# A two-layer encoder on one core: layer norms centred early on a partial mean, and two more tiles begun on the first half of the tokens

## The chip, the cores and the metric

The kernel runs on one core of one Trainium2 chip. A core has a matrix engine (PE, which multiplies a stationary 128x128 block with up to 512 moving columns and adds up in PSUM), three engines for elementwise work (VectorE or DVE, ScalarE or ACT, GpSimd or POOL) and SyncE (SP), which here issues the transfers. The metric is the device time of one execution in microseconds (us), the median of several runs.

## The reference

The input is 512 tokens of 1024 features in fp32; sixteen meta tokens go ahead of them, so 528 tokens run through two layers. Cut to what matters here:

```
h = layer_norm(concat(meta, x))
for l in range(2):
    cq, ckv, kr, lru_g, lru_x, g_mla, g_lru = split(h @ w_in[l])
    y_mla = attention(rms(cq), rms(ckv), rope(kr)) @ w_o_mla[l]
    y_lru = (gelu(lru_g) * rg_lru(dwconv(lru_x))) @ w_o_lru[l]
    z = sigmoid(g_mla) * y_mla + sigmoid(g_lru) * y_lru
    h = layer_norm(ALPHA * h + z @ w_out[l])
    gate, val = split(dwconv3(h @ w_up[l]))
    h = layer_norm(ALPHA * h + (gelu(gate) * val) @ w_down[l])
return h[16:]
```

`layer_norm` takes mean and variance over the 1024 features of a token, variance as the mean of the squared centred values. The hidden width of the second half is 2 x 2816; ALPHA is the constant weight of the residual.

## The kernel before

Features lie on the partitions: an activation is eight tiles x0 to x7 of 128 features by 528 tokens. Precision is kept by splitting every operand into a high part and a low rest (`split`: a cast, then a subtraction), so one block of weights times one tile is three matmuls, high x high, low x high and high x low (`unit`). A tile of 128 output features takes 8 blocks, for the two halves of the tokens (256 and 272, later 270 and 258 columns, as one PSUM bank holds 512) 48 matmuls. Weights come by DMA as `raw` in lots of 1024 columns, and are split on the chip into `whi` (ACT or DVE) and `wlo` (DVE or POOL); `Weights.take` does that.

All instructions are collected first and then put in order by a list planner (`Core.order`), which keeps PE's order as written, places the others by guessed costs and by times by which PE needs them, and picks the engine where an operation allows two ("VG": DVE or POOL). PSUM is a pool `d` of three double banks (`banks`, `pair`) and a pool `s` of two single banks (`bank`). In gaps that it expects, it places dummy matmuls (L361, `warm`).

A layer norm works across partitions: PE multiplies a tile with a matrix of ones, so that every partition gets the sum over all features. Three layer norms stand between two stages of matmuls; at these places the kernel works by halves of the tokens. `last_tiles` runs the last matrix ahead of the norm (w_out or w_down): tiles 0 to 3 over all tokens, then tiles 4 to 7 (`plt1`) for the first half, then for the second. `post` adds a finished tile to x, `add` adds x up in `lnsum`. After each half `ln_chunk` makes the norm: PE sums lnsum (bank `lnm`), eight centrings x - mean on DVE, eight squares on ACT, four additions, PE sums the squares (`lnv`), then eps, reciprocal and square root (`lnrs`), then per tile a scaling on DVE (g times lnrs), a cast to the high part (`h1h`; after w_down `h2h`) and the low part (`h1l`, `h2l`). Behind the norm `mtiles_by_chunk` begins the next stage with three tiles, first half of the tokens first: after w_out `pfg`, `pfv`, `pfg` (w_up), after w_down and at the start `pckv`, `pcq0`, `pcq1` (w_in). At the start the tokens' own norm (`ln0`) and its transposes (`ln0p`, from the input tiles `xin`) come in two halves too, the second popped from `later` after the first tile.

After pckv, pcq0 and pcq1 comes the tile `pkr` (the shared rotary key), times the tables cos and sin in `kra`, `krb`; then `rms` normalizes ckv and cq (`rrs`), and `rpa` is the first matmul tile on normalized queries. The tiles `pg` of the gates g_lru stand there as cover, others follow in the recurrent stage, whose order LRU_PLAN writes out ("L3" is g_lru's fourth tile). `conv3` and `ffn_post` make the hidden features f from a pair of tiles of w_up.

Of the kernel before, what the change touches and what calls it, by code (L numbers as in the profile page):

```python
# [43 lines left out]
            "L3 x6 O7 t2 x7 g4 y4 g5 y5 g6 g7 t3 y6 y7 l4 l5 l6 l7").split()  # L44
# [482 lines left out]
def trunk_kernel(ctx: ExitStack, tc: tile.TileContext, x, meta, wblk, vecs, rope, ident_in, lnf, out):  # L527
# [123 lines left out]
    for l in range(DEPTH):  # L651
# [45 lines left out]
        def ln_chunk(xs, s, c, g, b, hn):  # L697
            a, e = c
            n = e - a
            pm = bank("lnm")[:, :n]  # L700
            K.mm([(pm, ones, s[:, a:e], True, True)])
            K.act(small("dummy"), ones[:, 0:1], AF.Sqrt)
            qs = []
            for m in range(KD):
                xm = xs[m][:, a:e]
                K.stt(xm, pm, -1.0 / D, xm, ALU.mult, ALU.add)
                q = U("lnsq", F32, (128, n))
                K.act(q, xm, AF.Square)
# [4 lines left out]
            pv = bank("lnv")[:, :n]
            for m, q in enumerate(qs):
                K.mm([(pv, ones, q, m == 0, m == len(qs) - 1)])
            rs = U("lnrs", F32, (128, n))
            K.ts(rs, pv, 1.0 / D, LN_EPS, ALU.mult, ALU.add)
            K.recip(rs, rs)
            K.act(rs, rs, AF.Sqrt)
            for m in range(KD):  # L720
                xm = xs[m][:, a:e]
                hi, lo = hn[m][0][:, a:e], hn[m][1][:, a:e]
                K.stt(xm, xm, vec((g, l), m), rs, ALU.mult, ALU.mult)
                K.affine(hi, xm, 1.0, vec((b, l), m))
                K.stt(lo, xm, vec((b, l), m), hi.bitcast(F32), ALU.add, ALU.subtract)
            if g == "ln1_g":
                for m in range(KD):
                    K.affine(xs[m][:, a:e], xs[m][:, a:e], 1.0, vec((b, l), m))

        def last_tiles(name, xs, n_full, ks, kin, post, g, b, hn, cs):  # L730
# [51 lines left out]

        pss = [banks("pckv"), banks("pcq0"), banks("pcq1")]
        mtiles_by_chunk(pss, [kd("ckv", 0), kd("cq", 0), kd("cq", 1)], h, CF)
# [11 lines left out]
        pk = pair("pkr")  # L796
        mtile(pk, kd("kr", 0), h, CF)
        ta, tb = U("kra"), U("krb")
        K.tt(ta[0:64], pk[0:64], cos4[0:64], ALU.mult)
        K.tt(tb[0:64], pk[64:128], sin4[64:128], ALU.mult)  # L800
# [8 lines left out]
        sg, sg2, z1 = {}, {}, {}  # L809
# [174 lines left out]
        pre = chain([gate("g_lru", m, sg2) for m in range(3)])  # L984
# [124 lines left out]
        for m in range(KD):  # L1109
# [13 lines left out]
                   lambda m, ps, sl: residual(x1[m], ps, sl), "ln1_g", "ln1_b", hn, CQ)  # L1123
# [15 lines left out]
        def ffn_post(j, pg, pl):  # L1139
            sl = slice(FA, T)  # L1140
            tg = conv3(pg, j, "fg")
            K.act(tg[:, sl], tg[:, sl], AF.Gelu_apprx_tanh)
            tv = conv3(pl, NJ + j, "fv")
            K.tt(tg[:, sl], tg[:, sl], tv[:, sl], ALU.mult)
            f[j] = split_new(tg, "f", sl)

        def ffn_up(j):
# [8 lines left out]
        ffn_post(0, pg, pl)
        pl1 = pair("pfv")
        mtile(pl1, kd("w_up", NJ + 1), h, CQ)
        ffn_post(1, pg1, pl1)

        if not last:
# [9 lines left out]
            for j in range(2, PARTS[0].stop):  # L1171
                ffn_up(j)
            for p in range(1, 4):
# [7 lines left out]
                for j in PARTS[p - 1]:  # L1181
# [4 lines left out]
                       lambda m, ps, sl: K.tt(x1[m][:, sl], x1[m][:, sl], ps, ALU.add), "ln2_g", "ln2_b", hn, ((0, MIDS[1]), (MIDS[1], T)))  # L1186
# [64 lines left out]
        for j in range(2, NJ, 2):  # L1251
            ffn_up(j)
# [118 lines left out]
```

## Time and profile before

| | |
|---|---|
| median of 3 runs | 1839.12 us (1837.47 to 1840.18) |
| the profiled execution, its own time | 1835.23 us |
| its span, first to last instruction | 1833.5 us |
| PE busy | 97% of the span |
| DVE, ACT, POOL busy | 69%, 45%, 5% |
| mean granted clock of PE | 0.992 of full speed |
| HBM read | 146.75 MB, 81 GB/s over the span |

The views rest on one execution: busy shares, PE's list of waits (which instruction waited for whom, and how long), stretches of time with each engine's busy time, and the chain of waits, which goes back from the last instruction to what released it at each step. The clock is full speed (2.4 GHz) at 1.00; the lower level is 1.2 GHz. Busy shares mix stages with different limits, so single stretches matter more than the page's totals.

### The profile page before, as it was taken

The numbers are of one execution on the slowest core, as the hardware profiler recorded it, in microseconds if no ns is written. First come the engines' busy times: TensorE is split into PE (matmuls) and PEld (weight loads), VectorE is DVE, ScalarE is ACT, GpSimd is POOL, SyncE is SP. The second block draws the span as 40 slices with busy tenths as digits, with TensorE's granted clock in tenths as the row PEclk, the third lists the DMA queues.
The fourth block names the chain that finished last, engine by engine and source line by source line (L and its number), as shares of the span: only waits on it lengthen the run. The fifth ranks groups of instructions, "written<-read, shape, count | busy, mean of one in ns | idle before, by whom it ended". The sixth has DMA issues, their size and how long they took to land.

```text
span 1833.5 us, 33074 instructions
## 1 busy us (share of the span) xinstructions
PE 1785.7 (97%) x14068; PEld 1745.6 (95%) x14068; DVE 1266.5 (69%) x1923; ACT 821.5 (45%) x1330; POOL 88.1 (5%) x77
## 2 busy tenths in 40 slices
PE   7999999999999999999989999999999999999997
PEld 6999999999989999999979999999999899999997
DVE  6976757888586555555587767678875966666667
ACT  5556565574254333333245556655832632222222
POOL 0211000100010000000011100000000200000000
PEclk9999999999999999999989999999999999999999
DMA  5202122222213222222222121222222132222221
GB/s 194 70 26 81 58 72 90 84 97 86 93 58 104 93 93 84 95 88 93 93 75 65 51 66 47 93 93 92 82 93 92 60 122 96 91 95 93 92 93 46
DMA packets 46515, 155.25 MB, mean 85 GB/s; under 512 B 6016, under 2 KB 6656, under 8 KB 46368
## 3 DMA queue, kind: packets, MB, share of 16 engines
q1 hardware_dynamic: 46368, 153.14, 25.6%
q8 instruction: 110, 1.80, 0.4%
q14 instruction: 37, 0.30, 0.1%
HBM read 146.75 MB, written 2.10 MB: 81 GB/s over the span
## 4 chain that ended last, share of the span: by engine, by line
PE 90%; DVE 8%; ACT 2%; issue 1%; DMA 0%; SPq 0%; POOL 0%; DVEq 0%; ACTq 0%
PE pfv L386 14%; PE pfg L386 13%; PE pg L386 8%; PE plt L386 6%; PE pdt L386 6%; PE po L386 6%; PE px L386 5%; PE pol L386 5%; PE plg L386 5%; PE pdn L386 5%; PE sc L386 4%; PE pc L386 3%; PE ptp L395 1%; PE pcq L386 1%; DVE x L467 1%; PE pi L386 1%
## 5 line engine op out<-in xcount | busy, mean ns | idle before, releaser
L424 DVE TENSOR_TENSOR wlo<-raw,whi 128x1024 fp32r<-128x1024 f32 x256 | 311.3, 1221 | 67.0 <-ACT whi L411 61.7
L411 ACT CAST whi<-raw 128x1024 fp32r<-128x1024 f32 x201 | 209.4, 1047 | 246.6 <-PE plt L386 51.7
L386 PE MATMUL pfg<-h1l,whi 128*128 128x256 f32 (+2 forms) x704 | 200.3, 284 | 2.5 <-DVE h1l L467 2.5
L386 PE MATMUL pfg<-h1h,whi 128*128 128x256 f32 (+2 forms) x704 | 200.8, 285 | 1.5 <-ACT h1h L407 1.5
L386 PE MATMUL pfv<-h1h,whi 128*128 128x256 f32 (+2 forms) x704 | 199.9, 284 | 1.0 <-DVE fg L467 1.0
L386 PE MATMUL pfv<-h1l,whi 128*128 128x256 f32 (+2 forms) x704 | 199.4, 283 | 0.0
L386 PE MATMUL pfg<-h1h,wlo 128*128 128x256 f32 (+2 forms) x704 | 199.2, 283 | 0.0
L386 PE MATMUL pfv<-h1h,wlo 128*128 128x256 f32 (+2 forms) x704 | 198.9, 282 | 0.0
L467 DVE SCALAR_TENSOR_TENSOR fv<-pfv,vecs,fv 128x527 f32<-128x527 f32 (+1 forms) x88 | 66.7, 758 | 117.5 <-ACT fv L407 115.9
L386 PEld LDWEIGHTS pfg<-h1l,whi 128*128 128x128 f32 x704 | 133.2, 189 | 4.2 <-DVE h1l L467 3.2
L386 PEld LDWEIGHTS pfg<-h1h,whi 128*128 128x128 f32 x704 | 133.0, 189 | 2.7 <-ACT h1h L407 1.7
L386 PEld LDWEIGHTS pfv<-h1h,whi 128*128 128x128 f32 x704 | 132.7, 189 | 1.4 <-issue 1.4
L386 PEld LDWEIGHTS pfv<-h1l,whi 128*128 128x128 f32 x704 | 133.1, 189 | 0.0
L386 PEld LDWEIGHTS pfg<-h1h,wlo 128*128 128x128 f32 x704 | 133.0, 189 | 0.0
L386 PEld LDWEIGHTS pfv<-h1h,wlo 128*128 128x128 f32 x704 | 132.8, 189 | 0.0
L419 DVE CAST whi<-raw 128x1024 fp32r<-128x1024 f32 x70 | 48.5, 693 | 58.0 <-PE pfg L386 29.8
L467 DVE SCALAR_TENSOR_TENSOR fg<-pfg,vecs,fg 128x527 f32<-128x527 f32 (+1 forms) x88 | 66.5, 755 | 21.8 <-ACT fg L407 20.4
L407 ACT ACTIVATE p<-sc,mx 128x528 f32<-128x528 f32 (+2 forms) x68 | 47.8, 703 | 71.3 <-DVE mx L432 69.5
L407 ACT ACTIVATE fg<-pfg,vecs 128x528 f32<-128x528 f32 (+1 forms) x44 | 34.6, 786 | 100.3 <-PE pfg L386 100.3
L424 POOL TENSOR_TENSOR wlo<-raw,whi 128x1024 fp32r<-128x1024 f32 x15 | 36.9, 2461 | 832.3 <-ACT whi L411 832.2
L386 PE MATMUL pg<-h_hi,whi 128*128 128x256 f32 (+1 forms) x256 | 75.3, 294 | 0.7 <-DVE o_lo L424 0.7
L386 PE MATMUL pg<-h2h,whi 128*128 128x256 f32 (+1 forms) x256 | 74.7, 292 | 0.7 <-DVE o_lo L424 0.7
(371 smaller groups left out, 5833.1 us busy)
## 6 DMA issues: line engine op xcount, KB each, us to landing
raw<-in_wblk_dram SPq DMA_DIRECT2D x271, 512.0 KB, 3.5
xin<-in_x_dram SPq DMA_DIRECT2D x6, 256.0 KB, 4.7
out_dram<-ya SPq DMA_DIRECT2D x6, 256.0 KB, 2.1
lnf<-in_lnf_dram SPq DMA_DIRECT2D x4, 256.0 KB, 6.6
cos<-in_rope_dram SPq DMA_DIRECT2D x2, 264.0 KB, 5.8
sin<-in_rope_dram SPq DMA_DIRECT2D x2, 264.0 KB, 6.0
qs<-ra_hi SPq DMA_DIRECT2D x8, 66.0 KB, 2.0
qs<-rb_hi SPq DMA_DIRECT2D x8, 66.0 KB, 2.0
```

The source lines that it names most:

```text
L386: self.nc.tensor.matmul(out, lhsT=w, rhs=x, start=st, stop=sp)
L395: self.nc.tensor.transpose(o, i, d)
L407: return "A", cost * 1e-3, lambda: self.nc.scalar.activation(out, in_, func, **kw), table
L411: return "A", cost * 1e-3, lambda: self.nc.scalar.copy(out, in_), None
L419: return "V", self._v((out, a), 0, True), lambda: self.nc.vector.tensor_copy(out, a), None
L424: return eng, cost, lambda: e.tensor_tensor(out, a, b, op=op), None
L467: return self.vec(self._v((out, a, b), len(sc)), lambda: self.nc.vector.scalar_tensor_tensor(out, a, s, b, op0=op0, op1=op1), [out], [a, b ...
```

## The change

The layer norms at the three places compute the same by another way, and two further tiles join those that begin on the first half.

- In `last_tiles`, after the first of the four tiles of the first half, PE sums lnsum of tiles 0 to 3 for each half of the tokens (bank `lnc`). All eight x tiles and lnsum are centred on this mean of half of the features (for x4 to x7, to which the product is still to be added, divided by ALPHA where `post` multiplies by it). The squares of x0 to x3 are taken at once.
- `ln_chunk` takes the mean left (`lnm`), squares tiles 4 to 7 as they are, and gets the variance as the mean of the squares less the squared mean (`lnms`). Then come the reciprocal, the root, the centring on the mean left, the scaling, and g and b in one step, the result in x itself; `split` makes high and low from it. The dummy square root at its start is gone.
- `mtiles_by_chunk` takes two more tiles. Their first half of tokens goes into free columns of the double banks of the first two tiles, the second half into a single bank. After w_up's first three these are `w_up` NJ+1 and 2, whose convolution is made in parts (`take_up`); at the opening of a layer kr and the first g_lru tile, cut at 240 columns. `later` is popped after the whole first half.
- The transfers of the rotary tables are issued ahead of the opening; "L3" leaves LRU_PLAN, and three gates still stand ahead of `rms`, now the second to the fourth.

The diff, cut to its core:

```diff
-            "L3 x6 O7 t2 x7 g4 y4 g5 y5 g6 g7 t3 y6 y7 l4 l5 l6 l7").split()
+            "x6 O7 t2 x7 g4 y4 g5 y5 g6 g7 t3 y6 y7 l4 l5 l6 l7").split()
...
-        def mtiles_by_chunk(pss, descss, xs, chunks):
-            bl = [[W.take(d) for d in descs] for descs in descss]
-            for c in chunks:
+        def mtiles_by_chunk(pss, descss, xs, chunks, more):
+            bl = [[W.take(d) for d in descs] for descs in (*descss, *(x[0] for x in more))]
+            for i, c in enumerate(chunks):
...
-                    while later:
-                        later.pop()()
+                for (_, p0, parts, take), bs in zip(more, bl[len(pss):]):
+                    c = parts[i]
+                    ps = (bank("more") if i else p0)[:, :c[1] - c[0]]
+                    for k, b in enumerate(bs):
+                        unit(ps, b, xs[k], k == 0, k == len(bs) - 1, c)
+                    take(i, c, ps)
+                while later:
+                    later.pop()()
...
+        def squares(xs, c, to):
+            a, e = c
+            for x0, x1_ in zip(xs[::2], xs[1::2]):
+                q = [U("lnsq", F32, (128, e - a)) for _ in range(2)]
+                for t, x_ in zip(q, (x0, x1_)):
+                    K.act(t, x_[:, a:e], AF.Square)
+                K.tt(q[0], q[0], q[1], ALU.add)
+                to.append(q[0])
+
+        def ln_chunk(xs, s, c, qs, g, b, hn):
             a, e = c
             n = e - a
-            pm = bank("lnm")[:, :n]
+            pm, pv = bank("lnm")[:, :n], bank("lnv")[:, :n]
             K.mm([(pm, ones, s[:, a:e], True, True)])
-            K.act(small("dummy"), ones[:, 0:1], AF.Sqrt)
-            qs = []
+            sq = U("lnms", F32, (128, n))
+            K.act(sq, pm, AF.Square, scale=1.0 / D)
+            K.affine(sq, sq, -1.0, eps[:, 0:1])
+            squares(xs[KD - N_SPLIT:], c, qs)
+            for m, q in enumerate(qs):
+                K.mm([(pv, ones, q, m == 0, m == len(qs) - 1)])
+            K.stt(sq, pv, 1.0 / D, sq, ALU.mult, ALU.add)
+            K.recip(sq, sq)
+            K.act(sq, sq, AF.Sqrt)
+            for m in range(KD):
+                K.stt(xs[m][:, a:e], pm, -1.0 / D, xs[m][:, a:e], ALU.mult, ALU.add)
             for m in range(KD):
                 xm = xs[m][:, a:e]
-                K.stt(xm, pm, -1.0 / D, xm, ALU.mult, ALU.add)
...
+                K.tt(xm, xm, sq, ALU.mult)
+                K.affine(xm, xm, vec((g, l), m), vec((b, l), m))
+                split(xm, hn[m][0][:, a:e], hn[m][1][:, a:e])
...
+            qs = [[], []]
             for c in (0, 1):
...
+                    if not i:
+                        for d in ((0, 1) if not c else ()):
+                            da, de = cs[d]
+                            pc = bank("lnc")[:, :de - da]
+                            K.mm([(pc, ones, s[:, da:de], True, True)])
+                            for j in range(KD):
+                                K.stt(xs[j][:, da:de], pc, -1.0 / (128 * n_full * (1.0 if j < n_full else alpha)),
+                                      xs[j][:, da:de], ALU.mult, ALU.add)
+                            K.stt(s[:, da:de], pc, -1.0 / 128, s[:, da:de], ALU.mult, ALU.add)
+                            squares(xs[:n_full], cs[d], qs[d])
                     post(m, dst, slice(ca, ce))
                     add(m, slice(ca, ce))
-                ln_chunk(xs, s, cs[c], g, b, hn)
+                ln_chunk(xs, s, cs[c], qs[c], g, b, hn)
...
+        mtiles_by_chunk(pss, [kd("ckv", 0), kd("cq", 0), kd("cq", 1)], h, CF, [
+            (kd("kr", 0), pss[0], ((0, CUT), (CUT, T)), take_kr),
+            (win("g_lru", 0), pss[1], ((T0, T0 + CUT), (T0 + CUT, T)), take_gate)])
...
+        mtiles_by_chunk(pss, [kd("w_up", m) for m in (0, NJ, 1)], h, CQ, [
+            (kd("w_up", NJ + 1), pss[0], CQ, take_up("fv", NJ + 1)), (kd("w_up", 2), pss[1], CQ, take_up("fg", 2))])
```

Here is what DVE has in a row in the first layer's w_out (boundary 1 of the text below): x_870 to x_919 are the eight x tiles, plt the banks of single w_out tiles. Before, from the last residual of the first half to the sums of the squares:

```order
L467 SCALAR_TENSOR_TENSOR x_919<-x_919,plt_975 128x256
L424 TENSOR_TENSOR lnsum<-lnsum,x_919 128x256
L467 SCALAR_TENSOR_TENSOR x_870<-lnm,x_870 128x256
L467 SCALAR_TENSOR_TENSOR x_877<-lnm,x_877 128x256
L467 SCALAR_TENSOR_TENSOR x_884<-lnm,x_884 128x256
L467 SCALAR_TENSOR_TENSOR x_891<-lnm,x_891 128x256
L467 SCALAR_TENSOR_TENSOR x_898<-lnm,x_898 128x256
L467 SCALAR_TENSOR_TENSOR x_905<-lnm,x_905 128x256
L424 TENSOR_TENSOR lnsq<-lnsq 128x256
L467 SCALAR_TENSOR_TENSOR x_912<-lnm,x_912 128x256
L467 SCALAR_TENSOR_TENSOR x_919<-lnm,x_919 128x256
L424 TENSOR_TENSOR lnsq<-lnsq 128x256 x3
```

After, from the last weight split ahead of the first lnc on:

```order
L424 TENSOR_TENSOR wlo<-raw,whi 128x1024
L467 SCALAR_TENSOR_TENSOR x_898<-lnc,x_898 128x256
L467 SCALAR_TENSOR_TENSOR x_870<-lnc,x_870 128x256
L467 SCALAR_TENSOR_TENSOR x_877<-lnc,x_877 128x256
L467 SCALAR_TENSOR_TENSOR x_884<-lnc,x_884 128x256
L467 SCALAR_TENSOR_TENSOR x_891<-lnc,x_891 128x256
L467 SCALAR_TENSOR_TENSOR x_905<-lnc,x_905 128x256
L467 SCALAR_TENSOR_TENSOR x_912<-lnc,x_912 128x256
L467 SCALAR_TENSOR_TENSOR x_919<-lnc,x_919 128x256
L467 SCALAR_TENSOR_TENSOR lnsum<-lnc,lnsum 128x256
L467 SCALAR_TENSOR_TENSOR x_898<-x_898,plt_972 128x256
L424 TENSOR_TENSOR lnsq<-lnsq 128x256
```

The centrings moved from behind the first half's lnm to ahead of the residual of the first of its four tiles; lnsum is centred with them, and the second half's nine follow behind a sum of squares. Further on in the same stage, after, from the last residual of the first half on:

```order
L467 SCALAR_TENSOR_TENSOR x_919<-x_919,plt_985 128x256
L424 TENSOR_TENSOR lnsum<-lnsum,x_919 128x256
L424 TENSOR_TENSOR lnsq<-lnsq 128x256
L467 SCALAR_TENSOR_TENSOR x_870<-lnm,x_870 128x256
L467 SCALAR_TENSOR_TENSOR x_877<-lnm,x_877 128x256
L467 SCALAR_TENSOR_TENSOR x_884<-lnm,x_884 128x256
L467 SCALAR_TENSOR_TENSOR lnms<-lnv,lnms 128x256
L467 SCALAR_TENSOR_TENSOR x_891<-lnm,x_891 128x256
L467 SCALAR_TENSOR_TENSOR x_898<-lnm,x_898 128x256
L467 SCALAR_TENSOR_TENSOR x_905<-lnm,x_905 128x256
L467 SCALAR_TENSOR_TENSOR x_912<-lnm,x_912 128x256
L467 SCALAR_TENSOR_TENSOR x_919<-lnm,x_919 128x256
```

The counterpart before is the first piece above. Behind lnm now stand the centring on the mean left and one step that joins lnv and lnms; the second half's residuals begin among them.

PE at the end of the first layer's w_down (boundary 2), where f_hi and f_lo are the hidden features, h2h and h2l the first normalized ones. Before, at the second half's mean:

```order
L386 MATMUL plt_1402<-f_lo,whi 128x258
L386 MATMUL plt_1402<-f_hi,wlo 128x258
L361 MATMUL warm<-ones 128x128
L386 MATMUL lnm<-lnsum,ones 128x258
L386 MATMUL pckv<-h2h,whi 128x270
L386 MATMUL pckv<-h2l,whi 128x270
L386 MATMUL pckv<-h2h,wlo 128x270
L386 MATMUL pcq_1416<-h2h,whi 128x270
L386 MATMUL pcq_1416<-h2l,whi 128x270
L386 MATMUL pcq_1416<-h2h,wlo 128x270
```

After:

```order
L386 MATMUL plt_1407<-f_lo,whi 128x258
L386 MATMUL plt_1407<-f_hi,wlo 128x258
L386 MATMUL lnv<-lnsq,ones 128x258 x2
L361 MATMUL warm<-ones 128x128
L386 MATMUL lnm<-lnsum,ones 128x258
L386 MATMUL lnv<-lnsq,ones 128x258 x2
L386 MATMUL pckv<-h2h,whi 128x270
L386 MATMUL pckv<-h2l,whi 128x270
L386 MATMUL pckv<-h2h,wlo 128x270
L386 MATMUL pcq_1421<-h2h,whi 128x270
```

Half of the sums of squares moved ahead of the mean and the other half right behind it, where before three units of the next stage stood between lnm and lnv.

POOL from the recurrent stage of the first layer to the opening of the second (p, xc and y are names of the attention and the recurrent stage). Before:

```order
L432 TENSOR_SCALAR p<-p,sm 128x528 x6
L424 TENSOR_TENSOR xc_lo<-xc,xc_hi 128x528 x3
L424 TENSOR_TENSOR y_lo<-lg,y_hi 128x528
L424 TENSOR_TENSOR wlo<-raw,whi 128x1024 x5
L487 MEMSET PTt 80x528
L424 TENSOR_TENSOR wlo<-raw,whi 128x1024 x2
```

After:

```order
L424 TENSOR_TENSOR xc_lo<-xc,xc_hi 128x528 x3
L424 TENSOR_TENSOR y_lo<-lg,y_hi 128x528
L424 TENSOR_TENSOR wlo<-raw,whi 128x1024
L424 TENSOR_TENSOR h1l<-x_884,h1h 128x256
L424 TENSOR_TENSOR h1l<-x_891,h1h 128x256
L424 TENSOR_TENSOR h1l<-x_905,h1h 128x256
L424 TENSOR_TENSOR wlo<-raw,whi 128x1024
L424 TENSOR_TENSOR h2l<-x_884,h2h 128x270
L424 TENSOR_TENSOR h2l<-x_891,h2h 128x270
L424 TENSOR_TENSOR h2l<-x_912,h2h 128x258
L424 TENSOR_TENSOR wlo<-raw,whi 128x1024 x2
```

Six low parts of half a tile's tokens (h1l, h2l) moved to POOL here, and of its seven weight splits four stay; two more h1l follow at the second layer's w_out.

## Rows read from the trace of the kernel before

**Rows 1.** The page: busy time by engine; and DVE's weight split.

```profile
PE 1785.7 (97%) x14068; PEld 1745.6 (95%) x14068; DVE 1266.5 (69%) x1923; ACT 821.5 (45%) x1330; POOL 88.1 (5%) x77
...
L424 DVE TENSOR_TENSOR wlo<-raw,whi 128x1024 fp32r<-128x1024 f32 x256 | 311.3, 1221 | 67.0 <-ACT whi L411 61.7
```

**Rows 2.** PE's waits: waiting tile, releaser: total us, times, longest us.

```profile
PE lnm L386 <- DVE lnsum L424: 6.9, 1, 6.9
PE rpa L386 <- DVE c_lo L424: 4.5, 2, 3.1
PE lnv L386 <- DVE lnsq L424: 4.0, 5, 1.4
PE pfg L386 <- DVE h1l L467: 2.5, 2, 1.9
PE pi L386 <- ACT rr L407: 2.2, 3, 0.9
...
PE ln0p L395 <- DVE xin L432: 0.8, 1, 0.8
```

**Rows 3.** Stretches: us, busy of PE, PEld, DVE, ACT, POOL, PEclk, DMA, GB/s.

```profile
10.00:20.00 10.00, 8.54 (x51) 6.86 (x51) 9.88 (x29) 9.49 (x23) 0.00 (x0) 1.00 0.75 264
60.00:70.00 10.00, 7.40 (x39) 7.40 (x40) 9.91 (x9) 2.81 (x5) 4.74 (x3) 0.66 0.00 0
520.00:530.00 10.00, 8.14 (x65) 7.94 (x64) 9.97 (x14) 5.16 (x10) 2.46 (x1) 1.00 0.42 134
530.00:540.00 10.00, 8.23 (x57) 7.14 (x56) 9.87 (x27) 8.07 (x20) 2.39 (x1) 1.00 0.23 79
920.00:930.00 10.00, 3.47 (x30) 3.32 (x28) 9.93 (x12) 2.39 (x5) 5.39 (x4) 0.93 0.36 110
930.00:940.00 10.00, 9.10 (x33) 7.54 (x34) 7.96 (x22) 4.61 (x13) 0.00 (x0) 0.55 0.13 49
1430.00:1440.00 10.00, 7.92 (x54) 7.50 (x54) 9.51 (x13) 5.58 (x11) 5.74 (x4) 0.86 0.48 157
```

**Rows 4.** The chain of waits, boundary 1: start us, us, what.

```profile
501.68 12.51 PE plt L386 x105
...
518.54 1.31 PE lnv L386 x6
...
559.75 5.82 PE pfg L386 x48
```

**Rows 5.** The chain of waits, boundary 2.

```profile
900.50 12.01 PE plt L386 x96
...
955.15 5.91 PE pkr L386 x48
...
963.89 6.69 DVE rrs L475 x2
```

**Rows 6.** The chain of waits, boundary 3.

```profile
1409.95 12.98 PE plt L386 x108
...
1461.79 6.04 PE pfv L386 x48
```

**Rows 7.** DVE's timeline, boundaries 1 and 2: start us, us, instruction.

```profile
521.73 1.75 DVE L475 RECIPROCAL lnrs<-lnrs 128x256 f32<-128x256 f32 x1
...
913.00 2.17 DVE L467 SCALAR_TENSOR_TENSOR x<-lnm,x 128x270 f32<-128x270 f32 x6 [0.99 <-PE lnm L386]
...
917.84 2.58 DVE L424 TENSOR_TENSOR lnsum<-lnsum,x 128x258 f32<-128x258 f32 x1
```

**Rows 8.** POOL's timeline, boundary 2.

```profile
917.74 4.94 POOL L424 TENSOR_TENSOR wlo<-raw,whi 128x1024 fp32r<-128x1024 f32 x2 [384.41 <-ACT whi L411]
```

**Rows 9.** ACT's table loads between 500 and 560 us: busy us, mean ns.

```profile
L407 ACT ACT_TABLE_LOAD x2 | 2.6, 1283 | 0.0
```

More of the change, by code (lines that the diff above doesn't have):

```diff
@@ L713, in ln_chunk @@
[L713 to L730, printed above, removed]
+                K.tt(xm, xm, sq, ALU.mult)
+                K.affine(xm, xm, vec((g, l), m), vec((b, l), m))
+                split(xm, hn[m][0][:, a:e], hn[m][1][:, a:e])
+        def last_tiles(name, xs, n_full, ks, kin, post, g, b, hn, cs, alpha):
             s = U("lnsum")
@@ L781, in rms, with take_kr, take_gate @@
             return res
+        CUT = 240
+        kra, krb, sg_first = U("kra"), U("krb"), U("sg")
+        def take_kr(i, c, ps):
+            a, e = c
+            K.tt(kra[0:64, a:e], ps[0:64], cos4[0:64, a:e], ALU.mult)
+            K.tt(krb[0:64, a:e], ps[64:128], sin4[64:128, a:e], ALU.mult)
+        def take_gate(i, c, ps):
+            K.copy(sg_first[:, c[0]:c[1]], ps)
+        cos4, sin4 = U("cos4"), U("sin4")
+        K.dma(cos4, rope[0])
+        K.dma(sin4, rope[1])
         pss = [banks("pckv"), banks("pcq0"), banks("pcq1")]
[L784 removed]
+        mtiles_by_chunk(pss, [kd("ckv", 0), kd("cq", 0), kd("cq", 1)], h, CF, [
+            (kd("kr", 0), pss[0], ((0, CUT), (CUT, T)), take_kr),
+            (win("g_lru", 0), pss[1], ((T0, T0 + CUT), (T0 + CUT, T)), take_gate)])
         raws = []
@@ L795, in trunk_kernel @@
         krl = U("krl", F32R)
[L796 to L800, printed above, removed]
+        ta, tb = kra, krb
         K.tt(ta[0:32], ta[0:32], tb[0:32], ALU.subtract)
@@ L982, in head_out @@
             o.append(split_new(po, "o", TQ))
-        pre = chain([gate("g_lru", m, sg2) for m in range(3)])
+        pre = chain([gate("g_lru", m, sg2) for m in range(1, 4)])
         bg = chain([gate("g_mla", m, sg) for m in range(KD)])
@@ L1122, in trunk_kernel @@
         last_tiles("w_out", x1, KD - N_SPLIT, range(KD), z,
-                   lambda m, ps, sl: residual(x1[m], ps, sl), "ln1_g", "ln1_b", hn, CQ)
+                   lambda m, ps, sl: residual(x1[m], ps, sl), "ln1_g", "ln1_b", hn, CQ, ALPHA)
         h = hn
@@ L1150, in ffn_up, with take_up, take @@
             mtile(pl, kd("w_up", NJ + j), h, CQ)
-            ffn_post(j, pg, pl)
+            ffn_post(j, conv3(pg, j, "fg"), conv3(pl, NJ + j, "fv"))
+        parts = {}
+        def take_up(name, col):
+            t = U(name)
+            cw = lambda k: vec(("ffn_conv_w", l), k * 2 * NJ + col)
+            def take(i, c, ps):
+                a, e = max(c[0], FA), c[1]
+                K.affine(t[:, a:e], ps[:, a - c[0]:], cw(1), vec(("ffn_conv_b", l), col))
+                parts.setdefault(name, []).append((c, ps))
+                if not i:
+                    return
+                for (a, e), p in parts[name]:
+                    b, f = max(a + 1, FA, 1), min(e + 1, T)
+                    K.stt(t[:, b:f], p[:, b - 1 - a:f - 1 - a], cw(0), t[:, b:f], ALU.mult, ALU.add)
+                    b, f = max(a - 1, FA), e - 1
+                    K.stt(t[:, b:f], p[:, b + 1 - a:f + 1 - a], cw(2), t[:, b:f], ALU.mult, ALU.add)
+                parts[name] = t
+            return take
         pss = [banks("pfg"), banks("pfv"), banks("pfg")]
-        mtiles_by_chunk(pss, [kd("w_up", m) for m in (0, NJ, 1)], h, CQ)
+        mtiles_by_chunk(pss, [kd("w_up", m) for m in (0, NJ, 1)], h, CQ, [
+            (kd("w_up", NJ + 1), pss[0], CQ, take_up("fv", NJ + 1)), (kd("w_up", 2), pss[1], CQ, take_up("fg", 2))])
         pg, pl, pg1 = [t[:, 512 - MID:512 - MID + T] for t in pss]
[L1156 to L1159, printed above, removed]
+        ffn_post(0, conv3(pg, 0, "fg"), conv3(pl, NJ, "fv"))
+        ffn_post(1, conv3(pg1, 1, "fg"), parts["fv"])
+        pl = pair("pfv")
+        mtile(pl, kd("w_up", NJ + 2), h, CQ)
+        ffn_post(2, parts["fg"], conv3(pl, NJ + 2, "fv"))
         if not last:
@@ L1169, in down @@
                     K.tt(x1[m], x1[m], ps, ALU.add)
-            for j in range(2, PARTS[0].stop):
+            for j in range(3, PARTS[0].stop):
                 ffn_up(j)
```

24 lines of the change are left out of this document (7 added, 17 removed).

## The prediction

> **What bounds the kernel now.** I read the page's busy shares first: the matmul engine (PE) is busy for 1785.7 of 1833.5 us and VectorE (DVE) for 69% [rows 1]. So time can only be won where PE waits, runs at the lower clock, or multiplies for nothing. The list of PE's waits comes next [rows 2]: leaving out the first input, the long ones are the sums of the norms (lnm 6.9, lnv 4.0), the first normalized features (pfg <- h1l 2.5) and the first use of the normalized queries (rpa 4.5). All but the last sit at the three places where a layer norm stands between two long matmul stages; I call them boundary 1 (after the first w_out, near 500 to 560 us), 2 (after w_down, 900 to 961) and 3 (after the second w_out, 1410 to 1468). Stretches of 10 us show the engine on the other side [rows 3]: DVE is busy 9.97 and 9.87 of 10 us at 520 to 540 and 9.93 at 920 to 930, while PE drops to 8.1, 8.2 and 3.5. Two stretches also show PE's granted clock under one: 0.55 at 930 to 940, right after PE stood still, and 0.66 at 60 to 70. Those are mixtures of the 2.4 and the 1.2 GHz level.
>
> What a boundary loses is its extent less the work in it. A full tile of 48 matmuls takes 5.82 us, so a matmul is 0.121 us; three fp32 sums take 1.31 us, so a sum is 0.44 [rows 4].
> - Boundary 1 runs from 501.68 to 559.75 us: 58.1. Its work is eight tiles (four of w_out, four of w_up), 46.6, and ten sums, 4.4: 51.0. Lost: 7.1.
> - Boundary 2 runs from 900.50 to the end of pkr at 961.06: 60.6. Its work is four short tiles of w_down, 168 matmuls or 20.4, four tiles of 5.82 and the sums: 48.1. Lost: 12.4, the lower clock included [rows 5].
> - Boundary 3 runs from 1409.95 to 1467.83: 57.9. Work: 192 matmuls of w_out at the 0.120 of that stretch, 23.1, four tiles of 5.75, sums 4.4: 50.5. Lost: 7.4 [rows 6].
>
> Together 26.9 us.
>
> **The change, part by part.** *Early centring.* At each boundary two sums over the first four tiles (lnc) are added, one per half of the tokens, and for each DVE runs nine centrings. That is 6 x 0.44 = 2.6 us more for PE. A centring costs 0.35 us of DVE (six in 2.17, [rows 7]), so one lnc holds DVE for 9 x 0.35 = 3.15 us, 19 us over the kernel. They cost PE nothing as long as they lie beside matmuls: the order puts 27 to 30 of the second half's matmuls (27 x 0.121 = 3.3 us) behind each first lnc, 30 or more behind each second. Queued behind the centrings are the additions that empty the PSUM banks, of which the pool has two; cover is 3.3 against 3.15 plus a handover, so I take 0. If that cover is gone, each lnc costs up to its 3.15 us.
>
> *The path to the first normalized feature.* Before, the mean had to be taken off eight tiles, each squared, and the squares summed, in that order; now the squares of four tiles are ready beforehand and the variance needs one more step of DVE after the mean. What decides is a race between two queues that begin together at the end of the first half's lnm. In boundary 1 DVE runs 27 instructions up to the first h1l (the orders above show where they begin): a reciprocal 1.75, a weight split 1.22 [rows 1, 7], 25 short ones at 0.35, and 0.2 of handovers, 11.9 us. PE has 60 matmuls and seven sums, 10.3 us. PE waits 1.6. In boundary 2: 23 short ones and a reciprocal, 10.1, against 42 matmuls and seven sums, 8.2: PE waits 2.0. In boundary 3: 11.6 against 57 matmuls and seven sums, 10.0: PE waits 1.6.
>
> *ACT* gets eight more casts a half and does the squares of four tiles earlier; it is busy 2.4 to 8.1 of 10 us there [rows 3], so I cost that at nothing. A dummy that fetched the table of the square root early is dropped: the load, 1.28 us [rows 9], now stands straight ahead of the square root, beside DVE's reciprocal of 1.75 that the root waits for. It is hidden if ACT gets there in time; uncovered, six roots cost up to 7.7 us.
>
> *What is late next.* After four features DVE turns to the second half's centring (nine to eleven instructions, 3.2 to 3.9 us) while PE has 12 units of three matmuls, 4.3 us; the fifth feature is late by about 0.8, 0.5 and 1.1 us. *The two added tiles* then give PE 48 matmuls of the first half, 5.8 us, in which the second half's norm ends; before, this is where PE fell behind a second time. I take 0 further wait; the end without that cover is 5.8 us a boundary. Sum of what stays: 5.2 + 2.4 + 2.6 = 10.2, so 26.9 - 10.2 = 16.7 us are won.
>
> *The opening.* In layer 0 the tiles kr and g_lru join the first half, so its transposes of the second half no longer break in, and the fillers between the first matmuls and the 0.8 us wait for xin go [rows 2]. Their weight tiles and the rotary tables, 1.6 MB, are now issued ahead of the rest of x, which at 264 GB/s [rows 3] lands 6 us later; its statistics are queued behind the first half's splits on DVE, so that is hidden if it lands by about 17 us. I take 1.5 won, ends -3 (a late input) and +2.3. At rpa the two reciprocals (6.69 us, [rows 5]) still follow the sums with two gate tiles as cover, 11.7 us, but the slow splits that ran on POOL there are gone from its queue. The DVE chain is ten instructions over all tokens, at twice the 0.35 of a half, and the reciprocals: 13.7 us. A wait of 2 stays in place of the longest 3.1 in layer 0 [rows 2], without the lower clock (10 us at 0.66 is 3.4 us of matmuls not done): 3 won, ends 0 and 6. The third gate tile only moves: it leaves the LRU stage, where PE's waits are small (pi, 2.2 in three, [rows 2]). Walk: 16.7 + 1.5 + 3 = 21.2.
>
> *POOL beside DVE.* The order puts eight h-splits of half width on POOL among DVE's instructions with two SBUF inputs. The rows show such a meeting: POOL's weight split from 917.74, and beside it a DVE addition of 258 columns that takes 2.58 us where its neighbours take 0.35 to 0.4 [rows 7, 8]. Eight splits of a quarter of that length (0.6 us) can hold DVE for 4.8; the bounds are 0 and, at 2.4 each, 19. I take 4.8, by length: 21.2 - 4.8 = 16.4.
>
> The Trainium skill, in SBUF — State Buffer, section "Who interferes with whom", calls the port pair of these two engines an exclusive lock: the later instruction waits for the whole of the earlier one. The trace agrees, 2.58 us for the addition. By that rule alone the time would be the one with 4.8 taken off; without it, 4.8 us less.
>
> **The forecast.** The profiled execution took 1835.2 us, of which 1833.5 is the span; 1835.2 - 16.4 = 1818.8. The timed runs have a median of 1839.1, 3.9 above the profiled one, so I say 1823.
>
> **Rivals.**
> - *DVE stays the bound.* For it: DVE's 99% in rows 3, and some 90 more DVE instructions. Against it: 54 of them are centrings that fall before the mean, where DVE waits for PE. If the POOL meetings cost 1.5 us each in place of 0.6, 12 go from 21.2: 1830.
> - *The lower clock stays.* Waits of 1.6 to 2.0 us remain at each boundary, followed by shorter ones; before, no wait at boundary 3 was over 1.9 us [rows 2], and still 1430 to 1440 was granted 0.86; boundary 1 stayed at 1.00 [rows 3]. Three stretches like 60 to 70 cost 3 x 3.4 = 10 us: 1833.
> - *The centrings block the banks* (the slower side). If DVE reaches an lnc late, because a weight split (1.22 us) or a residual stands ahead of it, the bank is freed after PE's 27 matmuls are done. It decides from 0.3 us of lateness on. All six at full price cost 6 x 3.15 = 19, and the two waits a boundary bring the lower clock for 3.4 each: 29 against 21.2 - 4.8 won: 1852; with half of the banks' price, 1842.
> - *Nothing much:* the whole program is planned anew, so gains at the boundaries may be lost in the attention and LRU stages, for which no row speaks: 1839.
>
> **Chances.** Forecast 0.60, DVE bound 0.13, lower clock 0.09, banks 0.09, nothing 0.09. A measurement here can tell about 0.2%, 3.7 us. Faster: 0.60 + 0.13 + 0.08 = 0.81; same 0.10; slower 0.09. The range: below, the walk without POOL's price and without the first waits, 21.2 + 5.2 = 26.4 us, rounded to 1811; above, past DVE and clock, 1836, which leaves out the last two rivals.
>
> **What would show it.** In the changed profile the waits of PE on lnm before boundary 2 should be gone and the first pfg or pckv should wait 1 to 3 us for h1l or h2l; the granted clock should be 1.00 from 70 us to the end; lnc's centrings should lie where DVE was idle; the three boundaries, less a tile of 5.8, should be 4, 9 and 4 us shorter. A wait of PE for a bank at an lnc, or POOL splits beside DVE rows of over 1 us, would show me wrong, as would new waits in the stages between.

## The result and the profile after

The changed kernel takes 1815.88 us (1815.51 to 1817.32) against 1839.51 us (1837.47 to 1840.18): a ratio of 0.9875, interval 0.9858 to 0.9892, so 23.6 us less, where 16 were forecast. The profiled execution took 1815.5 us with a span of 1813.7, 19.7 under the span of before. Here is where those 19.7 lie, by the first matmul of each stage in the two traces. The 48 matmuls of g_lru's fourth tile ("L3"), which moved from the recurrent stage into each opening, are 5.8 us and are taken into account in the last column.

| stage, up to the first matmul of the next | before | after | won |
|---|---|---|---|
| opening of layer 0, to the first scores | 79.36 | 75.61 | 3.8 + 5.8 = 9.6 |
| attention, recurrence, to w_out | 398.67 | 393.22 | 5.5 - 5.8 = -0.3 |
| boundary 1, from w_out to w_down's first part | 128.11 | 126.65 | 1.5 |
| w_up and w_down, to w_down's last part | 273.70 | 274.31 | -0.6 |
| boundary 2, to the first scores of layer 1 | 111.94 | 108.10 | 3.8 + 5.8 = 9.6 |
| attention, recurrence, to w_out | 394.86 | 388.66 | 6.2 - 5.8 = 0.4 |
| boundary 3 and all behind it | 446.81 | 447.17 | -0.4 |

The opening and boundary 2 carry the gain; boundary 3, which had 7.4 us to win, gave none. The page's rows, as [rows 1], and PE's list of waits, as [rows 2], of the changed kernel:

```profile
PE 1780.0 (98%) x14065; PEld 1741.6 (96%) x14065; DVE 1272.8 (70%) x2006; ACT 828.8 (46%) x1340; POOL 81.0 (4%) x80
...
L424 DVE TENSOR_TENSOR wlo<-raw,whi 128x1024 fp32r<-128x1024 f32 x264 | 321.6, 1223 | 63.6 <-ACT whi L411 58.4
```

```profile
PE lnm L386 <- DVE lnsum L424: 3.4, 2, 1.7
PE pi L386 <- ACT rr L407: 3.1, 4, 0.9
PE lnv L386 <- DVE lnsq L424: 2.5, 3, 1.3
PE rpa L386 <- DVE c_lo L424: 1.7, 1, 1.7
...
PE pfg L386 <- DVE h1l L424: 0.5, 1, 0.5
```

The 6.9 for lnm is gone, but two waits of 1.6 to 1.7 on the second half's lnsum stand in its place, and one at rpa stays. DVE made eight weight splits more, since POOL now makes seven in place of fifteen. The stretches, as [rows 3]:

```profile
10.00:20.00 10.00, 9.88 (x67) 8.75 (x68) 9.39 (x19) 9.08 (x20) 0.00 (x0) 1.00 0.92 329
60.00:70.00 10.00, 10.00 (x84) 9.96 (x83) 9.56 (x14) 4.92 (x10) 4.18 (x3) 1.00 0.00 0
520.00:530.00 10.00, 7.26 (x50) 6.01 (x49) 9.92 (x27) 6.95 (x16) 3.21 (x4) 1.00 0.33 104
910.00:920.00 10.00, 8.47 (x58) 7.34 (x57) 9.90 (x26) 7.25 (x15) 3.07 (x2) 1.00 0.18 53
1410.00:1420.00 10.00, 8.15 (x60) 7.27 (x58) 10.00 (x18) 6.25 (x9) 2.49 (x1) 0.99 0.20 53
1420.00:1430.00 10.00, 9.35 (x53) 8.59 (x52) 10.00 (x26) 6.49 (x17) 1.59 (x2) 0.67 0.18 54
```

At 10 to 20 and 60 to 70 PE is now full and at its upper clock. At the boundaries it still drops to 7.3 to 8.5 of 10 us while DVE is full, and at 1420 the granted clock is 0.67. What DVE does there is seen when its timeline is laid beside POOL's (start us, us). POOL, boundaries 1, 2 and 3:

```profile
518.13 2.87 POOL L424 TENSOR_TENSOR wlo<-raw,whi 128x1024 fp32r<-128x1024 f32 x1 [167.42 <-ACT whi L411]
525.43 1.59 POOL L424 TENSOR_TENSOR h1l<-x,h1h 128x256 fp32r<-128x256 f32 x2 [4.43 <-ACT h1h L411]
...
911.10 2.40 POOL L424 TENSOR_TENSOR wlo<-raw,whi 128x1024 fp32r<-128x1024 f32 x1 [383.03 <-ACT whi L411]
...
960.57 2.48 POOL L424 TENSOR_TENSOR wlo<-raw,whi 128x1024 fp32r<-128x1024 f32 x1 [3.88 <-ACT whi L411]
...
1414.26 2.49 POOL L424 TENSOR_TENSOR wlo<-raw,whi 128x1024 fp32r<-128x1024 f32 x1 [165.50 <-ACT whi L411]
```

DVE at the same times, and (the one row of 961.04) two low parts ahead of rpa:

```profile
514.51 1.75 DVE L475 RECIPROCAL lnms<-lnms 128x256 f32<-128x256 f32 x1
...
518.70 2.57 DVE L424 TENSOR_TENSOR x<-x,lnms 128x256 f32<-128x256 f32 x1
...
525.77 2.87 DVE L467 SCALAR_TENSOR_TENSOR x<-lnm,x 128x272 f32<-128x272 f32 x8
...
910.28 1.81 DVE L467 SCALAR_TENSOR_TENSOR x<-lnm,x 128x270 f32<-128x270 f32 x5
...
961.04 3.16 DVE L424 TENSOR_TENSOR c_lo<-craw,c_hi 128x514 fp32r<-128x514 f32 x2 [0.23 <-ACT c_hi L411]
...
1414.42 2.61 DVE L424 TENSOR_TENSOR lnsq<-lnsq 128x258 f32<-128x258 f32 x1
```

A multiplication of 256 columns that takes 0.42 elsewhere takes 2.57 at 518.70 and ends (521.27) just behind POOL's split (521.00); the addition at 1414.42 takes 2.61 and ends behind the split of 1414.26. Both read two tiles in SBUF. The last of the five centrings at 910.28 run beside a split of POOL too (911.10), and the five take their usual 0.36 each: one of their inputs, lnm, is in PSUM. The eight centrings at 525.77 go undisturbed beside POOL's short splits for the same reason. So three weight splits on POOL stand right ahead of the three long waits of the list: lnm at boundaries 1 and 3, and rpa.

### The profile page after: what moved, and what is told of

It reads as the page before. It is cut to its first block, busy times and chain, and to the rows that moved or that the text cites. A ratio compares the mean times of both kernels' runs of the same rounds, so it can differ in the third digit from the quotient of the medians.

```text
span 1813.7 us, 33167 instructions
## 1 busy us (share of the span) xinstructions
PE 1780.0 (98%) x14065; PEld 1741.6 (96%) x14065; DVE 1272.8 (70%) x2006; ACT 828.8 (46%) x1340; POOL 81.0 (4%) x80
## 4 chain that ended last, share of the span: by engine, by line
PE 93%; DVE 5%; ACT 2%; issue 0%; DMA 0%; SPq 0%; POOL 0%; DVEq 0%; ACTq 0%
PE pfg L386 14%; PE pfv L386 14%; PE pg L386 8%; PE plt L386 6%; PE pdt L386 6%; PE po L386 6%; PE px L386 5%; PE pol L386 5%; PE plg L386 5%; PE pdn L386 5%; PE sc L386 4%; PE pc L386 3%; PE pcq L386 2%; PE ptp L395 1%; PE more L386 1%; PE pq L386 1%
## 5 line engine op out<-in xcount | busy, mean ns | idle before, releaser
L424 DVE TENSOR_TENSOR wlo<-raw,whi 128x1024 fp32r<-128x1024 f32 x264 | 321.6, 1223 | 63.6 <-ACT whi L411 58.4
L386 PE MATMUL pfg<-h1h,whi 128*128 128x256 f32 (+2 forms) x688 | 196.4, 285 | 0.0
L386 PE MATMUL pfg<-h1l,whi 128*128 128x256 f32 (+2 forms) x688 | 195.7, 284 | 0.5 <-DVE h1l L424 0.5
L386 PE MATMUL pfv<-h1h,whi 128*128 128x256 f32 (+2 forms) x688 | 195.6, 284 | 0.0
L386 PE MATMUL pfg<-h1h,wlo 128*128 128x256 f32 (+2 forms) x688 | 195.2, 284 | 0.0
L386 PE MATMUL pfv<-h1h,wlo 128*128 128x256 f32 (+2 forms) x688 | 195.0, 283 | 0.0
L407 ACT ACTIVATE fg<-pfg,vecs 128x512 f32<-128x512 f32 (+1 forms) x41 | 32.2, 785 | 102.0 <-PE pfg L386 102.0
L386 PE MATMUL plt<-z_hi,whi 128*128 128x256 f32 (+2 forms) x256 | 74.0, 289 | 0.0
L411 ACT CAST f_hi<-fg 128x528 fp32r<-128x528 f32 (+1 forms) x43 | 27.0, 628 | 101.9 <-DVE fg L424 101.7
L386 PE MATMUL po<-o_hi,whi 128*128 128x256 f32 (+2 forms) x256 | 72.7, 284 | 0.0
```

The source lines that it names most:

```text
L386: self.nc.tensor.matmul(out, lhsT=w, rhs=x, start=st, stop=sp)
L407: return "A", cost * 1e-3, lambda: self.nc.scalar.activation(out, in_, func, **kw), table
L411: return "A", cost * 1e-3, lambda: self.nc.scalar.copy(out, in_), None
L424: return eng, cost, lambda: e.tensor_tensor(out, a, b, op=op), None
```

## The experiments

All times are medians. The kernel before, run beside them, had 1838.7 to 1840.1 and scatters by 6 to 10 us, the others by 1 to 6. Ratios are to the kernel before beside them, with their intervals.

**The two halves of the change, each alone.** First the new norms without the rest, then the rest without the new norms:

```diff
 # norms alone: squares, ln_chunk and last_tiles as changed; mtiles_by_chunk, opening, w_up as before
-                ln_chunk(xs, s, cs[c], g, b, hn)
+                ln_chunk(xs, s, cs[c], qs[c], g, b, hn)
```

> The kernel before with the new norms alone (early centring, variance from the squares); opening and the tiles of w_up as before. If the gain of boundary 2 (about 9 us by the traces) is the norm's: 1828 to 1831. If it is that of the two added tiles as cover: 1834 to 1840, with a second row of waits after the first features. The opening stays as slow as before (the rpa wait of 3 us and its low clock stay).

```diff
 # tiles alone: the other way round
-        mtiles_by_chunk(pss, [kd("w_up", m) for m in (0, NJ, 1)], h, CQ)
+        mtiles_by_chunk(pss, [kd("w_up", m) for m in (0, NJ, 1)], h, CQ, [
...
```

> The changed kernel with the old norms: opening and the two added tiles alone. The traces put 9.5 us on the opening of the first layer, so 1830 if the tiles add nothing at the three boundaries; 1824 to 1827 if they cover the second half's norm there. If the parts simply add up, the gains of this and of the norms alone make 23.6 us together. If the POOL splits move by the plan alone, boundary 2 may change by 5 us either way.

Measured: norms alone 1834.4 (0.9967, 0.9954 to 0.9981), tiles alone 1825.9 (0.9925, 0.9909 to 0.9941). That is 4.4 and 12.8 us, 6 short of the 23.6 of both. In the trace of the norms alone, boundary 1 is 3.2 us longer and boundary 2 is 4.5 shorter; in that of the tiles alone they are 0.2 and 1.5 shorter (less the moved tile). The whole change has 1.5 and 9.6. Both times lie in the range that I had named for the added tiles as cover, but the runs with POOL pinned, below, say otherwise. These parts don't add up, so something that is in neither diff moves too.

**POOL's weight splits.** That something could be where the plan puts them. One edit keeps them on DVE, in the kernel before and in the changed one:

```diff
-            k.tt(lo, r, hi.bitcast(F32), ALU.subtract, "VG")
+            k.tt(lo, r, hi.bitcast(F32), ALU.subtract)
```

> The kernel before with one edit: the low part of the weights is always made on DVE, never on POOL (15 splits of 1.22 us more for DVE, spread over the program). Theory P: POOL's weight splits of 2.4 us hold DVE instructions with two SBUF inputs, and in the kernel before these holds stood on the chain at the boundaries (2.49, 2.20 and 2.88 us at boundary 2, 2.54 at 1, 1.64 and 2.87 at 3, 1.72 and 2.76 before rpa, each in place of about 0.35 to 0.7) - so without them about 12 to 15 us and part of the low clock are won: 1820 to 1828. Theory N, that the long way of the norm itself is what PE waits for: 1836 to 1843.

> The changed kernel with the same edit. In it three weight splits on POOL lie on the path: they hold one DVE instruction each for about 2.2 us longer at boundary 1, boundary 3 and before the second layer's rpa, PE then waits 1.6 to 1.7 us, and at boundary 3 the lower clock follows (6.8 us at half). Theory P: 3 x 1.6 and 3.4 of clock are won, 1808 (1806 to 1811), clock 1.00 at boundary 3. Rival, DVE is the bound there anyway: PE waits as before, 1814 to 1818.

Measured: before with the edit 1827.7 (0.9935, 0.9918 to 0.9952), after with it 1809.1 (0.9836, 0.9817 to 0.9854): 11.0 and 6.7 us won by a line that gives DVE 15 and 7 splits more. In the first kernel's trace the place of [rows 7, 8] has no POOL, and DVE's addition is short again:

```profile
917.53 0.43 DVE L424 TENSOR_TENSOR lnsum<-lnsum,x 128x258 f32<-128x258 f32 x1
```

There boundary 2, up to the first scores, takes 103.4 us in place of 111.9: 8.5 won without any change to the norm. The opening takes 74.3 in place of 79.4. At boundaries 1 and 3, where theory P had named holds too, nothing is won (0.2 and -0.5 us). In the changed kernel with the edit, the waits for lnm and most of that for rpa are gone from PE's list, and boundary 3 keeps the upper clock:

```profile
PE lnv L386 <- DVE lnsq L424: 2.7, 3, 1.3
...
PE rpa L386 <- DVE c_lo L424: 0.4, 1, 0.4
```

```profile
1405.00:1415.00 10.00, 10.00 (x74) 9.37 (x72) 9.22 (x22) 6.83 (x11) 0.00 (x0) 1.00 0.12 40
1415.00:1425.00 10.00, 9.04 (x68) 8.28 (x68) 10.00 (x27) 6.42 (x17) 1.61 (x2) 1.00 0.20 59
```

Both times lie in the ranges of theory P, which the first kernel bears out at boundary 2 and ahead of rpa; N falls as the account of boundary 2, and so does "DVE is the bound there anyway".

**The halves again, without POOL's weight splits.** The same two kernels as above, each with the line just shown; both start from the 1827.7.

```diff
+            k.tt(lo, r, hi.bitcast(F32), ALU.subtract)   # and: norms alone / tiles alone
```

> The kernel before with the weights' low parts on DVE alone and the new norms, nothing else; its base is the kernel before with that edit (1827.7). By boundaries of the two traces with that edit, the change is worth 3.5, 2.9 and 4.0 us there. If that is the norm's own: 1816 to 1819. If the added tiles are needed as cover for it, as boundary 1 of the norms alone suggests (3 us slower there): 1824 to 1830.

> The changed kernel with the weights' low parts on DVE alone and the old norms: opening and added tiles. Base 1827.7. The opening is worth 2.7 us by the two traces; if the tiles cover nothing with the old norms: 1824 to 1826. If the tiles are what shortens the boundaries: 1815 to 1819. With no holds by POOL the two parts should add up to the 18.6 us of the whole, if they don't need each other.

Measured: 1822.0 (0.9903, 0.9885 to 0.9922) and 1814.7 (0.9866, 0.9849 to 0.9883), 5.7 and 13.0 us. Now the two sum to 18.7, and the whole is 1827.7 - 1809.1 = 18.6. So, within the 1 to 5 us by which these kernels scatter, they don't need each other; it was the planning of POOL that mixed them. The 1822 lies between the two expectations, and neither for the tiles foresaw as much as 13.

**The opening.** Its part alone, and then that with the second half's norm and transposes popped after the first tile, as before:

```diff
 # opening alone (weights' low parts on DVE, old norms)
-        mtiles_by_chunk(pss, [kd("w_up", m) for m in (0, NJ, 1)], h, CQ, [
+        mtiles_by_chunk(pss, [kd("w_up", m) for m in (0, NJ, 1)], h, CQ, [])
 # and then, in mtiles_by_chunk, popped early
                         unit(ps[:, c[0]:c[1]], b, xs[k], k == 0, k == len(bs) - 1, c, spare)
+                    while later:
+                        later.pop()()
                 for (_, p0, parts, take), bs in zip(more, bl[len(pss):]):
...
-                while later:
-                    later.pop()()
```

> The kernel before with the weights' low parts on DVE alone and the new opening of a layer (kr and the first gate in the first half, tables early, L3 gone); old norms, no added tiles of w_up. Base 1827.7. By the profiled pair of the two kernels that differ in opening and tiles, the opening is worth 2.9 us and the tiles of w_up 5.8. But the same old opening lost another 5 us to the lower clock (20 to 34 us) in one profile and not in another. If the new opening also takes away that loss, which most timed runs of the old one then have: 1819 to 1822, all runs within 2 us. If not: 1824 to 1826.

> As the run with the new opening alone (1817.4, weights' low parts on DVE), but the second half's norm and transposes are popped after the first tile again, as in the kernel before; kr and the first gate still join the first half. If what the opening wins is the place of the transposes (the first half's units of pckv and pcq stand one behind the other, so PE has three tiles for each feature that comes, and no fillers and wait of 0.8 for xin): 1824 to 1828, runs up to 5 us apart. If it is the two tiles more in the first half, or one gate tile more ahead of rpa: 1817 to 1820.

Measured: 1817.4 (0.9882, 0.9863 to 0.9900) and 1826.2 (0.9926, 0.9913 to 0.9940). The opening is worth 10.3 of the 13.0, more than any expectation had, w_up's two tiles 2.8; and 8.7 of the 10.3 hang on where `later` is popped, since kr and the gate are in the first half in both. That line places the transposes, and at the three norms it also ends the stretch in which dummy matmuls may stand; of the 9.7 us between the two traces 7.4 lie in the opening and 2.3 behind it. The stretch of 20 to 34 us shows what differs in the opening. One row each of the kernel before with the edit, of the norms alone with it (where no edit touches the opening), of the opening alone and of the opening popped early:

```profile
20.00:34.00 14.00, 13.63 (x99) 12.06 (x100) 9.79 (x17) 8.81 (x20) 0.00 (x0) 1.00 0.42 147
```

```profile
20.00:34.00 14.00, 14.00 (x59) 11.40 (x59) 8.90 (x15) 8.17 (x18) 0.00 (x0) 0.51 0.32 114
```

```profile
20.00:34.00 14.00, 13.86 (x108) 12.27 (x107) 10.24 (x29) 9.14 (x17) 0.00 (x0) 1.00 0.32 107
```

```profile
20.00:34.00 14.00, 13.70 (x65) 11.43 (x66) 9.46 (x17) 8.16 (x18) 0.00 (x0) 0.63 0.37 121
```

The first two have the same opening; one got the upper clock there (99 matmuls), the other half of it (59 matmuls), and reached the first scores 5.0 us later. The runs of the first say which is the rule: the profiled one took 1823.7 at a mean clock of 0.995, four of the other five 1827.7 to 1827.9 at 0.993. With the new opening, PE has units of three tiles for each feature that arrives, is busy 9.88 of 10 us at 10 to 20 where it was 8.54 [rows 3], and all four runs of the opening alone lie within 1.8 us. That is most likely also why the medians differ by 23.6 and the two profiled spans by 19.7 (of its runs only the profiled one has a trace): the profiled execution of before had the upper clock at 20 to 34.

**The short splits on POOL.** The low parts of the normalized features, taken from POOL:

```diff
-                split(xm, hn[m][0][:, a:e], hn[m][1][:, a:e])
+                K.copy(hn[m][0][:, a:e], xm)
+                K.tt(hn[m][1][:, a:e], xm, hn[m][0][:, a:e].bitcast(F32), ALU.subtract)
```

> The changed kernel with the weights' low parts on DVE alone, and with the low parts of the normalized features at the three norms (the eight half-width splits that the plan puts on POOL) on DVE as well. Base 1809.1. My forecast took 4.8 us for POOL holding DVE in these: then 1804 to 1806. If the short splits hold nobody, eight more instructions of 0.35 us on DVE's queue cost 0 to 2.8: 1809 to 1812.

Measured 1813.2 (0.9859, 0.9842 to 0.9876), 4.1 us slower than the 1809.1. So these do not cost the 4.8 that the forecast took off; they win 4, more than the 2.8 of their DVE time. The traces show where. At boundary 1, without the short splits on POOL:

```profile
525.94 2.23 PE L361 MATMUL pfg<-ones 128*128 128x128 f32 x19
```

```profile
524.71 2.87 DVE L467 SCALAR_TENSOR_TENSOR x<-lnm,x 128x272 f32<-128x272 f32 x8
...
527.83 0.42 DVE L424 TENSOR_TENSOR h1l<-x,h1h 128x256 fp32r<-128x256 f32 x1
```

The plan puts the next low part behind the second half's eight centrings on DVE, and fills PE's time until then with 19 dummy matmuls; with the splits on POOL, which makes three low parts at that time, there are 3:

```profile
528.44 0.45 PE L361 MATMUL pfg<-ones 128*128 128x128 f32 x3
```

The three boundaries have 19, 17 and 19 dummies in place of 3, none and 3, and each is 1.7 us longer. PE's list of waits shows nothing of this, as PE isn't idle in it.

**The early centring.** Taken out, once with the weights' low parts on DVE alone and once as planned:

```diff
                     if not i:
                         for d in ((0, 1) if not c else ()):
-                            da, de = cs[d]
-                            pc = bank("lnc")[:, :de - da]
-                            K.mm([(pc, ones, s[:, da:de], True, True)])
-                            for j in range(KD):
-                                K.stt(xs[j][:, da:de], pc, ...)
-                            K.stt(s[:, da:de], pc, -1.0 / 128, s[:, da:de], ALU.mult, ALU.add)
                             squares(xs[:n_full], cs[d], qs[d])
```

> The changed kernel with the weights' low parts on DVE alone, and without the early centring: no lnc sums, no 54 centrings; the squares of the first four tiles are still taken early, of uncentred values, and the variance is the mean of the squares less the squared mean. Base 1809.1. If the centrings are hidden, as forecast, only the 6 sums on PE go, 6 x 0.44 = 2.6 us: 1806.5. If they hold up PE's banks (up to 19 us of DVE): 1795 to 1803. If DVE is freer and the plan merely moves: 1806 to 1810.

> The changed kernel without the early centring alone (no lnc sums, no 54 centrings; variance from the squares and the mean), weights' low parts on DVE or POOL as the plan likes. Base 1815.9. If the centrings cost as much as with those parts on DVE alone: 1807 (1805 to 1809). If they were hidden and only the six sums on PE go: 1813. If the holds by POOL's weight splits at boundaries 1 and 3 and before rpa set the time whatever else stands there: 1812 to 1815.

Measured: 1799.9 (0.9786, 0.9769 to 0.9803), 9.2 us under the kernel with the centring, and 1810.5 (0.9843, 0.9824 to 0.9861), 5.4 under the changed kernel. The first is the fastest of all. By size the first is the expectation of blocked banks, but in the trace with the centring PE has no wait at an lnc. The second lies between its expectations. Of the 8.5 us between the two traces with the weights' low parts on DVE, the six sums on PE are 2.6; PE's idle time at the three boundaries, which falls from 3.4 to 0.7, is another 2.7, and that is cover. The cause of the 3 us left (1.4 of them behind boundary 3) stays open. Here are the w_out matmuls of the second half between the first half's lnm and the second's sums at boundary 3, with the centring and without (columns as in [rows 3], without ACT and POOL):

```profile
1405.98:1413.60 7.62, 7.10 (x57) 6.98 (x57) 0.77 (x2) 1.00 0.01 3
```

```profile
1395.56:1407.50 11.94, 11.43 (x93) 11.31 (x93) 1.26 (x3) 1.00 0.15 46
```

The matmuls that PE does while DVE centres on lnc are the second half's. They were put ahead, and are missing behind the first half's lnm, where DVE has some 25 instructions to do: 57 are left of 93, 36 x 0.12 = 4.3 us (60 of 93 at boundary 1, 42 of 81 at boundary 2). DVE itself isn't faster there without the 54 centrings: from the first centring on lnm to the first low part it takes 11.1, 9.4 and 10.4 us with them and 10.1, 11.0 and 10.4 without. Without lnc PE's list has no wait for lnm or lnsq at all; of the norms only this is left:

```profile
PE pfg L386 <- DVE h1l L424: 0.4, 1, 0.4
```

With the weights planned freely, the gain is smaller. That trace has weight splits of POOL at 513.71, 910.92 and 1410.65, each with a long DVE row beside it (2.63, 2.28 and, for two instructions, 2.96 us), and PE waits three times for lnsum:

```profile
PE lnm L386 <- DVE lnsum L424: 4.3, 3, 1.6
...
PE rpa L386 <- DVE c_lo L424: 1.6, 1, 1.6
```

## Why the prediction was right, and where it was not

The sign and the range held: 1815.9 lies in 1811 to 1836, and the gain is 1.5 times the 16 forecast. (The lower end is rounded generously: 26.4 off 1839.1 is 1812.7.) Point by point the sum was less good than that, and that the total came near was partly luck: the opening won 5 us more than forecast, and boundaries 1 and 3 won 6.5 less. Two of the signs of being wrong that the prediction names came true: POOL splits stand beside DVE rows of over 1 us, and the granted clock is not 1.00 to the end. The wait of 1 to 3 us for the first low part, which it expected behind each norm, is a single 0.5; PE waits for the second half's lnsum instead.

- *The opening* was mis-sized most: 1.5 + 3 = 4.5 against 9.6 in the profiled pair. At 60 to 70 the forecast kept a wait of 2; there is none. The kernel before with its weight splits on DVE gets 5.1 of this by itself, so POOL holding DVE ahead of rpa is enough for about half of it, without the order of the tiles. In the first 34 us the forecast counted fillers and a wait of 0.8 us. It had no term for the lower clock there, because the one execution shown did not have it; most timed runs of that kernel with its weight splits on DVE do, another 4 to 5 us.
- *Boundary 2* came out as the sum said, 9.6 (rpa included) against 12.4 - 2.0 - 0.5 - 0.9 = 9.0, but for another reason: 8.5 of it goes if POOL merely leaves the weight splits alone. The rows that I read for the price of POOL [rows 7, 8] were at the same time the cause of the stall that I ascribed to the long norm. In the changed kernel a split still stands there (911.10), but beside centrings, which it doesn't hold.
- *Boundaries 1 and 3*: 3.8 each were forecast by the race of the two queues, 1.5 and nothing came. In each a weight split on POOL added 2.2 us to DVE's queue, and at boundary 3 the clock then fell: half clock from 1419.8 to 1426.7, the rival "the lower clock stays", at one place of three. Its condition, a wait of 1.6 to 2.0 with shorter ones behind it, doesn't decide it: boundary 1 had the same wait of 1.7 and kept 1.00.
- *The price of POOL* was 4.8, and the splits cost 6.7. The size is near by luck, the instruction was wrong: I priced the eight short splits, which win 4.1, and left out the seven long ones. The order showed four of these around the boundaries.
- *The centrings at nothing* is the step that failed outright. The cover for each lnc was there, 27 to 30 matmuls, and no bank was blocked. But the cover was taken from the place where the next wait needed it. I counted 60 matmuls behind lnm in the race of boundary 1 without asking how many there would be without lnc. The centring costs 9.2 us with the weights' low parts on DVE alone and 5.4 in the kernel as planned, 2.6 of them on PE; the forecast had only these 2.6.
- *The table of the square root* was hidden as said, shown here at boundary 1: its load runs from 515.07 to 516.35, beside the reciprocal of 514.51 to 516.26.

```profile
515.07 1.28 ACT L407 ACT_TABLE_LOAD   x1
```

With POOL's weight splits out of both, the change is worth 18.6 us: 10.3 the opening, 2.8 the tiles of w_up, 5.5 the norms (1814.7 - 1809.1), which would be 14.7 without their early centring. What is shown for the lower clock in the opening is that it goes with the place of the transposes. That PE's idle time and fillers at 10 to 20 us bring it is not shown: in the five traces with the transposes early, PE is busy 8.54, 8.65 and 9.36 of these 10 us where the upper clock follows at 20 to 34, and 8.85 and 8.91 where it doesn't.

The Trainium skill, in SBUF — State Buffer, section "Who interferes with whom", says that a DVE instruction with two SBUF inputs contends with a GpSimd instruction that reads SBUF, and one with at most one SBUF input, outside DVE's 2-port modes, does not. The traces agree on both: 2.57 and 2.61 us for the first kind, 0.36 each for the centrings beside the split of 911.10. By that sentence the instructions to keep away from a split can be read off the order of a kernel.

## What to carry to other kernels

Cover is a stock: matmuls put behind one wait are missing behind the next, so an added step that is "hidden" has to be charged at the place where its cover came from. When a planner orders everything anew, compare the two kernels with its free choices pinned (here one engine choice) before a gain or loss is put down to the edit. An instruction on a helper engine that is cheaper for the main one can still cost more than it saves when it holds the main one for its whole length at a place where others wait. A planner's dummy matmuls hide waits from PE's list of waits, so their number is to be compared too.

## What the hardware showed that I had not expected

- A weight split on POOL of 2.4 to 2.9 us holds one DVE instruction with two SBUF inputs until it is over, 2.2 us more than its own 0.4. One with a PSUM input beside it isn't held at all (five in 1.81 us, the last of them beside a split). With all weight splits on DVE the kernel before takes 11 of its 1839 us less.
- The short splits hold too where they meet such an instruction: in the run without lnc and with the weights planned freely, DVE rows of 0.98 and 0.95 us stand beside POOL splits of 0.73 and 0.83 at 1417 and 1418. In the changed kernel most of them met centrings.

```profile
1417.26 0.98 DVE L424 TENSOR_TENSOR x<-x,lnms 128x256 f32<-128x256 f32 x1
...
1418.50 0.95 DVE L424 TENSOR_TENSOR h1l<-x,h1h 128x256 fp32r<-128x256 f32 x1
```

- The same instructions in the first 34 us are granted the upper clock in one execution and half of it in another, 5 us apart. The eight kernels with the transposes behind the first half scatter by 0.8 to 3.7 us from run to run, the others by 3.4 to 10.
